# Rotating an 8192 x 8192 matrix: 16 KB load pieces and merged store reads in place of 4 KB pieces

## The chip, the cores and the metric

One core of one Trainium2 chip runs the kernel. The metric is the time of one execution on the device, in microseconds (us). All times are medians of several executions; readings of a profile are from one of these executions.

Ratios are computed as the mean time of one kernel's runs over the mean of the other kernel's runs in the same rounds, so they are not quite the ratio of the medians quoted beside them.

## The reference

```python
x = np.random.randn(8192, 8192).astype(np.float32)   # 268.4 MB
def reference(x, k):          # k == 1
    return np.rot90(x, k)     # out[i, j] = x[j, 8191 - i]
```

A rotation moves data and computes nothing. Each byte must be read once and written once: 268.4 MB in and 268.4 MB out.

## The kernel before

Rotating means transposing and reversing. The kernel loads rows into SBUF, reverses each group of 128 columns on VectorE (DVE), transposes 128 x 128 blocks on TensorE (PE) into PSUM, copies from PSUM to SBUF on ScalarE (ACT), and stores. Loads are issued on the SP queue, stores on the ACT queue; the same 16 DMA engines serve both.

```python
QT = 4; PT = 4; S = 512; K = 2
# a_pool, r_pool, o_pool: 3 buffers each, of 16 KB per partition; psum: 2 buffers
for RB2 in range(n_rb2):
    for CB2 in range(n_cb2):                    # macro tile of 1024 x 1024
        for t in range(K):                      # a load: 512 rows x 1024 columns, 2 MB
            a_big = a_pool.tile([P, QT, K * S], dt, tag="a_big")
            src = x[...].rearrange("(q r) c -> r q c", q=QT)
            nc.sync.dma_start(out=a_big[:], in_=src)          # 4 KB pieces
            ar_big = r_pool.tile([P, QT, K * S], dt, tag="ar_big")
            nc.vector.tensor_copy(out=ar_big..., in_=a_big...[:, :, ::-1])
        for s in range(K):
            o_big = o_pool.tile([P, PT, K * S], dt, tag="o_big")
            for t in range(K):
                # ... 16 transposes into psum_t ...
                nc.scalar.copy(o_big[:, :, t * S : (t + 1) * S], psum_t[:])
            dst = out[...].rearrange("(p m) f -> m p f", p=PT)
            nc.scalar.dma_start(out=dst, in_=o_big[:])        # 4 KB pieces
```

A "piece" here is one contiguous run that a DMA moves: in this kernel 1,024 floats, 4 KB, on both sides of every load and every store.

## Time and profile before

| | before |
|---|---|
| time | 1286.25 us (1285.63 to 1286.27) |
| PE, ACT, DVE busy | 56%, 37%, 23% |
| DMA busy | 0.9 or more in all but the last slice |
| rate in mid-span | 421 GB/s, flat |

The first fence is from the page of the kernel before. In the slices, each digit is the busy share of one fortieth of the span in tenths, and the GB/s line has the rate of the same slices. Section 3 has packets, MB and packet time as a share of the 16 engines' span for each queue: q1 holds the loads, q10 the stores.

```profile
DMA  9999999999999999999999999999999999999998
GB/s 382 422 421 421 421 421 422 421 421 421 421 421 421 421 421 421 421 422 421 420 421 421 421 421 421 421 421 421 422 420 420 421 421 422 421 421 421 421 421 361
DMA packets 135208, 537.48 MB, mean 418 GB/s; under 512 B 4096, under 2 KB 4096, under 8 KB 135168
q1 hardware_dynamic: 67584, 268.44, 50.9%
q10 hardware_dynamic: 67584, 268.44, 50.9%
DMA 88%; DVE 8%; PE 2%; ACT 1%; issue 0%; DVEq 0%; SPq 0%
a_big<-in_x_dram SPq DMA_DIRECT2D x128, 2048.0 KB, 27.4
out_dram<-o_big ACTq DMA_DIRECT2D x128, 2048.0 KB, 26.1
```

The kernel is bound by DMA. No slice but the last has free DMA time, no compute engine is busy for even 60% of the span, and the chain of work that ended last is 88% DMA. The 67,584 packets per queue are 65,536 data packets of 4,096 B and 2,048 completion writes. So only two things can make it faster: a higher rate of the DMA engines while they run, and less idle time at the two ends.

### The profile page before, as it was taken

How to read it: one execution, taken by the hardware profiler on the slowest of the kernel's cores; microseconds unless marked ns; L12 is line 12 of the kernel's file. 1: busy time of each engine (PE TensorE's matmuls, PEld its weight loads, DVE VectorE, ACT ScalarE, POOL GpSimd, SP SyncE). 2: the span in 40 equal slices, each digit the busy share in tenths (PEclk: the TensorE clock that was granted, in tenths of full speed). 3: DMA queues.
4: the chain of work that ended last, by engine and by line, in shares of the span. 5: the costliest groups of instructions: out<-in, count | busy, mean ns of one | idle time of the engine just before them, and what ended most of it. 6: DMA issues, size and time to landing. Idle time of an engine off the chain costs nothing.

```text
span 1284.6 us, 9394 instructions
## 1 busy us (share of the span) xinstructions
PE 718.8 (56%) x4096; PEld 662.7 (52%) x4096; DVE 293.6 (23%) x128; ACT 471.1 (37%) x257; POOL 0.7 (0%) x6
## 2 busy tenths in 40 slices
PE   5465564556555565456554565555646556465553
PEld 5455464555544555456454464555645456455553
DVE  2222222222222222222222222222222222222221
ACT  3334433343333433343333433334333343334433
POOL 0000000000000000000000000000000000000000
PEclk9666766776767767776777767767677766776776
DMA  9999999999999999999999999999999999999998
GB/s 382 422 421 421 421 421 422 421 421 421 421 421 421 421 421 421 421 422 421 420 421 421 421 421 421 421 421 421 422 420 420 421 421 422 421 421 421 421 421 361
DMA packets 135208, 537.48 MB, mean 418 GB/s; under 512 B 4096, under 2 KB 4096, under 8 KB 135168
## 3 DMA queue, kind: packets, MB, share of 16 engines
q1 hardware_dynamic: 67584, 268.44, 50.9%
q10 hardware_dynamic: 67584, 268.44, 50.9%
q8 instruction: 32, 0.52, 0.1%
q14 instruction: 8, 0.07, 0.0%
HBM read 268.44 MB, written 268.44 MB: 418 GB/s over the span
## 4 chain that ended last, share of the span: by engine, by line
DMA 88%; DVE 8%; PE 2%; ACT 1%; issue 0%; DVEq 0%; SPq 0%
DMA a_big<-in_x_dram 88%; DVE ar_big L60 8%; PE psum_t L76 2%; ACT o_big L81 1%; DVEq L60 0%; SPq L55 0%
## 5 line engine op out<-in xcount | busy, mean ns | idle before, releaser
L76 PE MATMUL psum_t<-ident,ar_big 128*128 128x128 f32 x4096 | 718.8, 354 | 552.7 <-ACT o_big L81 354.4
L76 PEld LDWEIGHTS psum_t<-ident,ar_big 128*128 128x128 f32 x4096 | 662.7, 188 | 608.5 <-ACT o_big L81 389.5
L81 ACT COPY o_big<-psum_t 128x2048 f32<-128x2048 f32 x256 | 469.9, 1868 | 801.5 <-DMA out_dram<-o_big 771.6
L60 DVE COPY ar_big<-a_big 128x4096 f32<-128x4096 f32 x128 | 293.6, 2294 | 970.6 <-DMA a_big<-in_x_dram 816.4
L81 ACT ACT_TABLE_LOAD x1 | 1.3, 1283 | 0.7 <-PEq L104 0.7
masks.py:199 POOL TENSOR_SCALAR_AFFINE_SELECT ident<-ident 128x128 f32<-128x128 f32 x1 | 0.3, 292 | 0.1
masks.py:197 POOL MEMSET ident<- 128x128 f32 x1 | 0.2, 204 | 0.3 <-POOLq L104 0.3
L104 POOL MEMSET const-bfloat16-1.0<- 128x1 bf16 x1 | 0.1, 102 | 0.0
L104 POOL MEMSET const-uint8-127<- 128x1 uint8 x1 | 0.1, 102 | 0.0
L104 POOL MEMSET const-float32-0.0<- 128x1 f32 x1 | 0.1, 98 | 0.2 <-issue 0.2
L104 POOL MEMSET const-float32-1.0<- 128x1 f32 x1 | 0.1, 98 | 0.0
## 6 DMA issues: line engine op xcount, KB each, us to landing
a_big<-in_x_dram SPq DMA_DIRECT2D x128, 2048.0 KB, 27.4
out_dram<-o_big ACTq DMA_DIRECT2D x128, 2048.0 KB, 26.1
```

The costliest lines, as they stand in the source:

```text
L60: nc.vector.tensor_copy(out=ar_big.rearrange("r q (b m) -> r (q b) m", m=P), in_=rev_src,)
L76: nc.tensor.transpose(psum_t[:, w, q * P : (q + 1) * P], ar_big[:, q, col0 : col0 + P], ident,)
L81: nc.scalar.copy(o_big[:, :, t * S : (t + 1) * S], psum_t[:])
L104: nc = _bacc.Bacc("TRN2", target_bir_lowering=False, num_devices=1)
```

## The change

The intent is fewer and larger DMA pieces. A macro tile is now 512 rows x 4096 columns, so a load fetches 16 KB of one row per partition in one piece. Stores shrink to 1 MB, four output rows of 2 KB per partition. The four rows lie side by side in SBUF, and a hook that runs over the finished program rewrites the store's source so that the 8 KB are read as one piece, while the destination keeps four rows of 2 KB.

```diff
+R = 512
+C = 4096
+RT = R // P          # 4 row tiles
+G = 2048 // R        # 4 column blocks to a store
+def whole_reads(nc):
+    ...               # for each DMA instruction:
+    ap = [list(d) for d in src.ap]
+    if len(ap) == 3 and ap[2][0] == 1 and ap[1][0] == ap[2][1]:
+        ap = [ap[0], [1, 1], [1, ap[1][1] * ap[2][1]]]
+        block.instructions[n] = copy.replace(
+            ins, ins=[copy.replace(src, ap=ap)], ant_dge_precooked=False)
...
-    a_pool bufs=3, r_pool bufs=3, o_pool bufs=3          (16 KB each)
+    a_pool bufs=2 (16 KB), r_pool bufs=2 * RT (16 KB), o_pool bufs=5 (8 KB)
...
+    for r0 in range(0, N, R):
+        for c0 in range(0, M, C):
+            for t in range(RT):
+                a = a_pool.tile([P, C], dt, tag="a")
+                nc.sync.dma_start(out=a[:], in_=x[r0 + t*P : r0 + (t+1)*P, c0 : c0 + C])
+                ar = r_pool.tile([P, C], dt, tag="ar")      # reversed by DVE as before
+            for g0 in range(0, CG, G):
+                o = o_pool.tile([P, G, R], dt, tag="o")
+                # ... 16 transposes, one ACT copy of [128, 2048] ...
+                dst = out[top : top + G*P, r0 : r0 + R].rearrange("(g m) f -> m g f", g=G)
+                nc.scalar.dma_start(out=dst, in_=o[:])
```

The counts of matmuls (4096), DVE copies (128) and ACT copies (256) stay. Stores go from 128 of 2 MB to 256 of 1 MB.

More of the change, by code (lines that the diff above doesn't have):

```diff
@@ L2 @@
+import copy
 from contextlib import ExitStack
@@ L10 @@
 P = 128
+R = 512
+C = 4096
+RT = R // P
+CG = C // P
+G = 2048 // R
+PW = 2048 // R
+def whole_reads(nc):
+    for fn in nc.m.functions:
+        for block in fn.blocks:
+            for n, ins in enumerate(block.instructions):
+                if not isinstance(ins, mybir.InstDMACopy):
+                    continue
+                src = ins.ins[0]
+                ap = [list(d) for d in src.ap]
+                if len(ap) == 3 and ap[2][0] == 1 and ap[1][0] == ap[2][1]:
+                    ap = [ap[0], [1, 1], [1, ap[1][1] * ap[2][1]]]
+                    block.instructions[n] = copy.replace(
+                        ins,
+                        ins=[copy.replace(src, ap=ap)],
+                        ant_dge_precooked=False,
+                    )
 @with_exitstack
@@ L22 @@
     assert k == 1, f"only k=1 supported, got {k}"
+    nc.at_finalize(whole_reads)
     N, M = x.shape
     dt = x.dtype
-    QT = 4
-    PT = 4
-    S = 512
-    K = 2
-    n_rb2 = N // (K * S)
-    n_cb2 = M // (K * S)
     consts = ctx.enter_context(tc.tile_pool(name="consts", bufs=1))
@@ L37 @@
     make_identity(nc, ident)
-    a_pool = ctx.enter_context(tc.tile_pool(name="a_pool", bufs=3))
-    r_pool = ctx.enter_context(tc.tile_pool(name="r_pool", bufs=3))
-    o_pool = ctx.enter_context(tc.tile_pool(name="o_pool", bufs=3))
-    psum_pool = ctx.enter_context(tc.tile_pool(name="psum", bufs=2, space=bass.MemoryType.PSUM))
-    for RB2 in range(n_rb2):
-        for CB2 in range(n_cb2):
-            c_base = CB2 * K * S
-            r_base = RB2 * K * S
-            ar_list = []
-            for t in range(K):
-                a_big = a_pool.tile([P, QT, K * S], dt, tag="a_big")
-                src = x[
-                    r_base + t * S : r_base + (t + 1) * S, c_base : c_base + K * S
-                ].rearrange("(q r) c -> r q c", q=QT)
-                nc.sync.dma_start(out=a_big[:], in_=src)
-                ar_big = r_pool.tile([P, QT, K * S], dt, tag="ar_big")
-                nblk = QT * K * S // P
-                rev_src = a_big.rearrange("r q (b m) -> r (q b) m", m=P)[:, :, ::-1]
+    a_pool = ctx.enter_context(tc.tile_pool(name="a_pool", bufs=2))
@@ new lines @@
+    r_pool = ctx.enter_context(tc.tile_pool(name="r_pool", bufs=2 * RT))
+    o_pool = ctx.enter_context(tc.tile_pool(name="o_pool", bufs=5))
+    psum_pool = ctx.enter_context(
+        tc.tile_pool(name="psum", bufs=2, space=bass.MemoryType.PSUM)
+    )
+    for r0 in range(0, N, R):
+        for c0 in range(0, M, C):
+            rows = []
+            for t in range(RT):
+                a = a_pool.tile([P, C], dt, tag="a")
+                nc.sync.dma_start(
+                    out=a[:], in_=x[r0 + t * P : r0 + (t + 1) * P, c0 : c0 + C]
+                )
+                ar = r_pool.tile([P, C], dt, tag="ar")
@@ L60 @@
                 nc.vector.tensor_copy(
-                    out=ar_big.rearrange("r q (b m) -> r (q b) m", m=P),
-                    in_=rev_src,
-                )
-                ar_list.append(ar_big)
-            for s in range(K):
-                cb = K * CB2 + s
-                o_big = o_pool.tile([P, PT, K * S], dt, tag="o_big")
-                for t in range(K):
-                    psum_t = psum_pool.tile([P, PT, QT * P], mybir.dt.float32)
-                    ar_big = ar_list[t]
-                    for p in range(PT):
-                        w = PT - 1 - p
-                        col0 = s * S + p * P
-                        for q in range(QT):
+                    out=ar.rearrange("r (b m) -> r b m", m=P),
@@ L76 @@
+                    in_=a.rearrange("r (b m) -> r b m", m=P)[:, :, ::-1],
+                )
+                rows.append(ar)
+            for g0 in range(0, CG, G):
+                o = o_pool.tile([P, G, R], dt, tag="o")
+                for h in range(0, G, PW):
+                    ps = psum_pool.tile([P, PW, R], mybir.dt.float32)
+                    for w in range(PW):
+                        col = (g0 + h + w) * P
+                        for t in range(RT):
                             nc.tensor.transpose(
-                                psum_t[:, w, q * P : (q + 1) * P],
@@ L78 @@
-                                ar_big[:, q, col0 : col0 + P],
+                                ps[:, PW - 1 - w, t * P : (t + 1) * P],
+                                rows[t][:, col : col + P],
                                 ident,
                             )
-                    nc.scalar.copy(o_big[:, :, t * S : (t + 1) * S], psum_t[:])
-                top = N - S - cb * S
-                dst = out[top : top + S, r_base : r_base + K * S].rearrange(
-                    "(p m) f -> m p f", p=PT
+                    nc.scalar.copy(o[:, G - PW - h : G - h, :], ps[:])
@@ L86 @@
+                top = M - c0 - (g0 + G) * P
+                dst = out[top : top + G * P, r0 : r0 + R].rearrange(
+                    "(g m) f -> m g f", g=G
                 )
-                nc.scalar.dma_start(out=dst, in_=o_big[:])
+                nc.scalar.dma_start(out=dst, in_=o[:])
 _INS = ['x', 'k']
```

## The prediction

> **What bounds it now.** The 16 DMA engines. The page's slices show a DMA busy share of 0.9 or more throughout and a flat 421 GB/s from the second slice to the last but one; PE is busy 56%, ACT 37%, DVE 23% of the span. The chain of waits is 88% load DMA. So only the rate per DMA engine and the idle DMA at both ends count.
>
> **The rate, from the trace's packet records.** All data packets are 4,096 B. One takes 159 ns, a completion write 9 ns. While only the load queue runs (the first 23 us of data) the rate is 410 GB/s, which is 16 x 2 MB/(32 x 159 + 9 ns): packets follow each other without overlap. With both queues running, 421 GB/s means one 4 KB packet per 155.8 ns on each engine. The Trainium skill, "DMA: Bandwidth & Descriptors", section "Where 436 GB/s comes from", gives a ceiling of 435.2 GB/s, or 150.6 ns per 4 KB; its section "Why small descriptors are slow" names a fixed cost per packet. This trace agrees with both: 5.2 ns over the ceiling with two queues, 8.4 ns with one. An 8,192 B instruction-fetch packet took 307 ns at the start, under 2 x 159.
>
> **What the change does.** Matmuls (4096), DVE copies (128) and evictions (256, 1.87 us) stay as they are. Loads stay 128 x 2 MB, but in 16 KB pieces rather than 4 KB. Stores become 256 x 1 MB: 8 KB read pieces, but 2 KB output rows. 128 more store issues (0.38 us each) go to ACT, which has 800 us idle: free.
>
> Sum per 4 KB with two queues, if the cost is per read piece: loads 150.6 + 5/4, stores 150.6 + 5/2, some 0.2 for completions: mean about 152.7 ns against 155.8, 2.0% less. 8,192 x 3.1 ns = 25 us, all on the critical path. I take off about 3 us: a 16 KB load packet against an 8 KB store packet should give loads the larger share, so they run ahead, fill their buffers and leave stretches in which only stores run, at the dearer one-queue cost. Ends: the first store comes about 7 us later (four loads, not two, go first), but loads fill that time; the tail ends in smaller stores. Both near zero. Compute keeps pace in store-only stretches: 16 transposes take 1.97 us at full clock, an ACT copy with its issue about 2.3 us, a 1 MB store about 2.5 us. At half clock 16 transposes take 3.6 us, but five output buffers cover that.
>
> If the cost is per written piece instead, stores take 150.6 + 10, the mean is about 156.4 ns, and the time is 1290 to 1303.
>
> **Prediction: 1263 us, 80% range 1247 to 1294. Faster by over 2%: 0.40; within 2%: 0.52; slower by over 2%: 0.08.**
>
> **What would show it.** Right: steady rate 428 to 431 GB/s; fewer, larger packets (16 KB loads near 610 ns, not four of 159); loads share above half in some slices; DMA still 0.9 or more in every slice; the chain still DMA; PE, ACT and DVE totals unchanged. Wrong: rate at or below 421 GB/s, store packets of 2 KB at 80 ns or more each; or DMA gaps in mid-span with ACT waiting for PE at half clock.
>
> **What would make it wrong.** 2 KB output rows that cost HBM or the write side more than 4 KB rows; a 16 KB row still cut into 4 KB pieces, so that nothing is gained on loads; load buffers (two, not three) leaving the load queue empty after each 2.3 us DVE copy while stores cannot fill the gap; coarser macro tiles (8 MB) making loads and stores alternate; a real ceiling under 435 GB/s, so that little of the 5 ns is recoverable.

## The result, and the profile after

| | before | after |
|---|---|---|
| median | 1285.98 us (1285.63 to 1286.27, 4 runs) | 1279.92 us (1278.93 to 1282.31, 4 runs) |
| ratio | | 0.9955, 95% interval 0.9941 to 0.9969 |
| rate, 200 to 1100 us | 420.9 GB/s | 423.8 GB/s |
| lost at both ends against that rate | 7.4 us | 9.9 us |

The change is faster by 0.45%, where 1.8% was forecast. The third row is bytes moved in 200 to 1100 us of the span, from the trace's packet records. The fourth is the span less the time that all bytes would take at that rate.

The same lines of the page, for the changed kernel:

```profile
DMA  9999999999999999999999999999999999999998
GB/s 364 424 425 424 426 423 424 426 425 424 424 425 427 422 426 424 424 426 426 422 422 425 422 425 424 422 422 424 427 417 427 420 423 426 417 428 421 425 422 352
DMA packets 55339, 537.51 MB, mean 421 GB/s; under 512 B 6144, under 2 KB 6144, under 8 KB 6144
q10 hardware_dynamic: 36864, 268.45, 50.5%
q1 hardware_dynamic: 18432, 268.44, 49.6%
DMA 91%; PE 4%; ACT 3%; issue 0%; DVE 0%; ACTq 0%; SPq 0%
a<-in_x_dram SPq DMA_DIRECT2D x128, 2048.0 KB, 12.7
out_dram<-o ACTq DMA_DIRECT2D x256, 1024.0 KB, 20.9
```

Three readings. The pieces are what the change wanted: 16,384 load packets of 16 KB and 32,768 store packets of 8 KB (36,864 less 4,096 completion writes), so a store with four output rows does count as one packet. The rate rose by under 1% only, and it is no longer flat: slices go from 417 to 428 GB/s. And a load now lands 12.7 us after its issue, not 27.4, while a store still needs 20.9 us for half of the bytes: the loads get more than their share.

The share can be read from the DMA view of single stretches. This is the changed kernel from 622 to 646 us of the span (packets, MB, share of the 16 engines):

```profile
q1 hardware_dynamic: 437, 6.39, 62.8%
q10 hardware_dynamic: 511, 3.73, 37.4%
```

and this is the same view from 653 to 661 us:

```profile
q10 hardware_dynamic: 461, 3.36, 101.2%
q1 hardware_dynamic: 1, 0.00, 0.0%
```

With both queues running, loads move nearly twice the bytes of stores. Then no load runs at all. The Trainium skill, "DMA: Bandwidth & Descriptors", section "Queues, rings and completion order", says that each DMA engine takes turns between the queues that have work, a packet at a time. This trace agrees: packets of 16 KB against packets of 8 KB give 6.39 against 3.73 MB. The records do not name the engine, but they can be chained into 16 engines, because each one starts a few ns before another ends. In the chains of the changed kernel from 200 to 1100 us, 8,868 of some 10,200 unbroken runs of load records on one engine are a single record, so a turn here is one piece. The loads run ahead until their buffers are full, and the view of waits shows on what they then wait (engine, line, what it waited for: us in total, times, longest). Before:

```profile
DVE ar_big L60 <- DMA a_big<-in_x_dram: 816.4, 108, 8.6
DVE ar_big L60 <- PE psum_t L76: 154.2, 20, 8.6
```

After:

```profile
DVE ar L83 <- DMA a<-in_x_dram: 500.6, 71, 10.9
DVE ar L83 <- PE ps L96: 443.0, 30, 21.2
```

The DVE copy now waits 443 us for PE to free row buffers, up to 21.2 us at a time; while it waits, no load buffer comes free.

Sorting the span by microseconds, from the packet records with each packet's bytes spread over its time: in the changed kernel 726 us have both queues at about 2:1 and run at 426.0 GB/s, 292 us have stores alone at 418.7, and 220 us lie between at 420.7. In the kernel before, 1223 us have both queues at 1:1 and run at 420.4. The bounds between these sorts are a choice; other bounds move them by some tens of us.

### The profile page after: what moved, and what is told of

The parts are those of the page before. It is cut to its first block, busy times and chain, and to the rows that moved or that the text cites. A ratio compares the mean times of both kernels' runs of the same rounds, so it can differ in the third digit from the quotient of the medians.

```text
span 1278.2 us, 9636 instructions
## 1 busy us (share of the span) xinstructions
PE 708.0 (55%) x4096; PEld 641.3 (50%) x4096; DVE 291.2 (23%) x128; ACT 479.0 (37%) x257; POOL 0.7 (0%) x6
## 3 DMA queue, kind: packets, MB, share of 16 engines
q10 hardware_dynamic: 36864, 268.45, 50.5%
## 4 chain that ended last, share of the span: by engine, by line
DMA 91%; PE 4%; ACT 3%; issue 0%; DVE 0%; ACTq 0%; SPq 0%
DMA out_dram<-o 90%; PE ps L96 4%; ACT o L101 3%; DMA a<-in_x_dram 2%; DVE ar L83 0%; ACTq L107 0%; ACTq L101 0%; SPq L77 0%
## 5 line engine op out<-in xcount | busy, mean ns | idle before, releaser
L96 PE MATMUL ps<-ident,ar 128*128 128x128 f32 x4096 | 708.0, 348 | 557.2 <-ACT o L101 531.6
L96 PEld LDWEIGHTS ps<-ident,ar 128*128 128x128 f32 x4096 | 641.3, 183 | 623.5 <-ACT o L101 596.2
L101 ACT COPY o<-ps 128x2048 f32<-128x2048 f32 x256 | 477.7, 1868 | 787.4 <-DMA out_dram<-o 708.7
L83 DVE COPY ar<-a 128x4096 f32<-128x4096 f32 x128 | 291.2, 2293 | 943.6 <-DMA a<-in_x_dram 500.6
## 6 DMA issues: line engine op xcount, KB each, us to landing
a<-in_x_dram SPq DMA_DIRECT2D x128, 2048.0 KB, 12.7
out_dram<-o ACTq DMA_DIRECT2D x256, 1024.0 KB, 20.9
```

Of the source, the lines that this page charges most:

```text
L83: nc.vector.tensor_copy(out=ar.rearrange("r (b m) -> r b m", m=P), in_=a.rearrange("r (b m) -> r b m", m=P)[:, :, ::-1],)
L96: nc.tensor.transpose(ps[:, PW - 1 - w, t * P : (t + 1) * P], rows[t][:, col : col + P], ident,)
L101: nc.scalar.copy(o[:, G - PW - h : G - h, :], ps[:])
```

## The experiments

Two theories stood at the start. **Cuts**: the forecast counted only read pieces, and each row that a store piece is cut into on the write side costs too. **Alternation**: loads of 16 KB and stores of 8 KB drive each other into stretches with one queue, which the forecast took off at 3 us. A third was that compute and the coarse macro tile hold the rate down.

### The store reads not merged

```diff
-    nc.at_finalize(whole_reads)
```

> The changed kernel without the merging of the store reads: each store reads 2 KB pieces as it writes 2 KB rows. Theory A (the fixed cost is per read piece, about 5 ns with two queues and 8.4 ns with one): store records of 2 KB at about 84 ns, loads get 8/9 of the mixed rate, store-only rate near 2048*16/84 = 390 GB/s, time 1305 to 1335 us. Theory B (the cost is per written piece, so merging reads bought nothing): time within 0.3% of the changed kernel, about 1280 us, and store-only rate still near 418 GB/s.

Measured: 1330.24 us, ratio 1.034 (1.0322 to 1.0357), right result.

```profile
DMA packets 153643, 537.51 MB, mean 404 GB/s; under 512 B 6144, under 2 KB 6144, under 8 KB 137216
q10 hardware_dynamic: 135168, 268.45, 53.0%
q1 hardware_dynamic: 18432, 268.44, 48.9%
```

A store packet of 2 KB takes 84 ns in the packet records, four of them 336 ns; the merged packet of 8 KB took 314 ns. So the cost follows read pieces for the most part, as the forecast had it, and merging is worth 50 us here: without it the change would have been a loss of 3.4%. Not all of the 50 us is the price of pieces: with packets of 2 KB against 16 KB, the records show about 480 us of stores alone at about 400 GB/s.

### Loads in 8 KB pieces

```diff
-nc.sync.dma_start(out=a[:], in_=x[r0 + t*P : r0 + (t+1)*P, c0 : c0 + C])
+for j in range(0, C, 2048):
+    nc.sync.dma_start(out=a[:, j : j + 2048], in_=x[..., c0 + j : c0 + j + 2048])
```

> The changed kernel with each load row fetched as two DMAs of 8 KB pieces, so that load and store packets are equal. Theory A (alternation: 16 KB load packets against 8 KB store packets give loads two thirds, they run ahead, and the 292 us of store-only stretches at 418.7 GB/s follow): shares go to one half each, store-only time in mid-span falls under 60 us, rate near the 426 GB/s of the mixed stretches nearly all the time, 1266 to 1273 us. Theory B (alternation is harmless, the size of the load piece is what counts): 8 KB load pieces cost 1.3 ns more per 4 KB of load, time 1281 to 1287 us.

Measured: 1281.03 us, ratio 0.9962 (0.9947 to 0.9977), right result. The store-only time fell from 292 to 32 us and the rate became even (most slices 422 to 425), yet the time is that of the changed kernel. Theory B's number came out. As the cuts below show, it is not its reason alone: here the cuts are what is left to see.

### Macro tiles of 1024 x 2048

```diff
-R = 512
-C = 4096
+R = 1024
+C = 2048
-    a_pool bufs=2
+    a_pool bufs=4
```

> Macro tiles of 1024 rows x 2048 columns: 8 KB load pieces, 8 KB store reads, output rows of 4 KB rather than 2 KB. Against the run with 8 KB loads and 2 KB output rows this changes the length of the written row. Theory A (a cut on the write side adds cost: the 8 KB store record of 315 ns over 309 ns in the first stretch is that cut): store records near 310 ns and 0.3 to 1% faster than the run with 2 KB rows, about 1258 to 1268 us. Theory B (written pieces are free): the same time as that run within 0.2%.

Measured: 1279.04 us, ratio 0.9944 (0.9929 to 0.9958), right result. Store records fell to 310 ns, as theory A said, but the time came down by 0.15% only, which is theory B's time. From 100 to 500 us the rate was 426.6 GB/s; from 1100 to 1200 us it was 418.1, and 12.0 us were lost at the ends.

### Stores in 16 KB pieces

```diff
-G = 2048 // R          # o_pool bufs=5, r_pool bufs=2 * RT
+G = 4096 // R          # o_pool bufs=3, r_pool bufs=2 * RT - 1
```

> The changed kernel with stores of 2 MB that read 16 KB pieces for eight 2 KB rows, so both queues move 16 KB packets (3 output buffers of 16 KB, 7 row buffers). Theory A (alternation costs, and the cost is per read piece): equal shares, hardly any store-only stretch, rate 427 to 431 GB/s, 1256 to 1268 us. Theory B (alternation harmless): only the saving per store piece, about 1 ns per 4 KB of store, 1274 to 1279 us. If the write cuts dominate: store records of 16 KB near 628 ns, no gain over the run with 8 KB loads.

Measured: 1280.40 us, ratio 0.9957 (0.9936 to 0.9977), right result. The shares are even and the mid-span rate is 425.5 GB/s, under the forecast. Store records are 624.6 ns against 613 for loads of the same size: eight rows of 2 KB cost. The plain copy with the same pieces and rows, below, has 426.0, so the cuts explain the rate. 14.6 us were lost at the ends, against 7.1 in that copy.

### Plain copies: the queues without compute

To settle the sum, four kernels copy instead of rotating. They share 12 buffers of 16 KB between loads and stores and use no compute engine. Their outputs are wrong, which doesn't matter for the times.

```diff
+for each block of 128 x 4096 floats:
+    a = pool.tile([P, 4096], dt, tag="a")          # 12 buffers
+    nc.sync.dma_start(out=a..., in_=x...)          # pieces of 4, 8 or 16 KB
+    nc.scalar.dma_start(out=out..., in_=a...)      # the same pieces, or rows of 2 KB
```

> No rotation: a plain copy of the input with no compute, so the result is wrong on purpose; it measures the two DMA queues by themselves. Pieces of 4 KB both ways, shapes as in the kernel before. If compute and its waits cost the kernel before nothing in mid-span, the mid-span rate is again 421 GB/s (155.7 ns per 4 KB on each engine).

> Plain copy, wrong on purpose: pieces of 8 KB both ways, no cuts. Theory A (a fixed cost of 5.2 ns per piece with two queues over a ceiling of 435 GB/s): 153.2 ns per 4 KB, 428 GB/s in mid-span. Theory B (some ceiling near 426 GB/s binds whatever the piece): at most 426 to 427 GB/s, and the 16 KB copy the same.

> Plain copy, wrong on purpose: pieces of 16 KB both ways, no cuts. Theory A (fixed cost per piece): 151.9 ns per 4 KB, 431 GB/s in mid-span. Theory B (a ceiling near 426 GB/s): 426 to 427 GB/s, no more than with 8 KB pieces.

> Plain copy to rotated block places, wrong on purpose: loads of 16 KB pieces, stores that read 16 KB and write eight 2 KB rows. Theory of the cuts (each cut of a store piece costs about 1.9 ns, as the 624.6 ns against 612 ns records of the run with 16 KB stores suggest): store records 622 to 627 ns against 611 in the 16 KB copy without cuts, mid-span rate 1% below that copy. Rival (the longer store records come from compute or from waiting for the load queue, not from the cuts): the same rate and records as the 16 KB copy.

The fences show the stretch from 200 to 1100 us of the 4 KB, the 8 KB and the 16 KB copy, and of the 16 KB copy whose stores write eight rows of 2 KB, in this order. The last two numbers of a line are the DMA share and GB/s.

```profile
200.00:1100.00 900.00, 0.00 (x0) 1.00 1.02 422
```

```profile
200.00:1100.00 900.00, 0.00 (x0) 1.00 1.01 428
```

```profile
200.00:1100.00 900.00, 0.00 (x0) 1.00 1.01 431
```

```profile
200.00:1100.00 900.00, 0.00 (x0) 1.00 1.01 426
```

| copy | time | mid-span | per 4 KB on one engine |
|---|---|---|---|
| 4 KB both ways | 1281.05 us | 421.5 GB/s | 155.5 ns |
| 8 KB both ways | 1262.88 us | 428.0 GB/s | 153.1 ns |
| 16 KB both ways | 1253.21 us | 431.3 GB/s | 152.0 ns |
| 16 KB, stores in eight 2 KB rows | 1268.58 us | 426.0 GB/s | 153.8 ns |

The last column is 16 x 4,096 B over the rate. The first three rows fit one line: 150.8 ns plus 4.7 ns per piece (155.5, 153.15 and 152.0). The forecast's piece cost (5.2 ns over 150.6) was right, and theory A of these runs holds; there is no lower ceiling near 426 GB/s. The cuts are right too: eight written rows instead of one cost 15 us of time.

### Is it the cut, or the short row? And the cuts taken out of the changed kernel

```diff
 # 16 KB copy: four rows of 4 KB instead of eight of 2 KB
-top, left = n // 16 * 1024, n % 16 * 512      # g=8
+top, left = n // 8 * 512, n % 8 * 1024        # g=4
```

> The plain copy with 16 KB store reads, now written as four 4 KB rows instead of eight 2 KB rows (wrong on purpose). Theory A (a price per cut, 13.1 ns over seven cuts): three cuts give records of 616 to 617 ns and 429 GB/s in mid-span. Theory B (short rows of 2 KB are what is slow, 4 KB rows are free): records of 611 ns and 431 GB/s.

Measured: 1257.45 us, 429.7 GB/s, store records of 614.8 ns (611 uncut, 624.1 with eight rows). Its output is wrong, which doesn't matter for the time. From the rates, the pair of a load and a store piece takes 2 x 16,384 x 16/rate: 1215.7 ns uncut, 1220.1 with three cuts, 1230.7 with seven. That is 1.5 ns per cut with 4 KB rows and 2.1 ns with 2 KB rows. Most of it goes by the cut, and short rows add to it: between the theories, nearer to A.

```diff
 # changed kernel: each store writes its 8 KB in one piece; wrong on purpose
-dst = out[top : top + G*P, r0 : r0 + R].rearrange("(g m) f -> m g f", g=G)
-nc.scalar.dma_start(out=dst, in_=o[:])
+nc.scalar.dma_start(out=out[top : top + P, left : left + 2048],
+                    in_=o.rearrange("m g f -> m (g f)"))
```

> The changed kernel, in which each store writes its 8 KB per partition as one piece to a contiguous place rather than as four 2 KB rows; the result is wrong on purpose, everything else (macro tiles, loads, buffers, compute) is as in the changed kernel. Theory A (three cuts per store piece cost 4 to 6 ns and take back about half of the gain): mid-span rate 426 to 428 GB/s, store records near 309 rather than 314 ns, 1266 to 1272 us. Theory B (the gain went into the alternation of loads and stores and into the ends, not the cuts): within 0.3% of the changed kernel, 1277 to 1283 us.

Measured: 1279.05 us (1275.55 to 1282.69), ratio 0.9944 (0.9919 to 0.997). **Theory A failed here.** The cuts cost less when taken away, as far as that goes: store records fell from 314.3 to 310.8 ns and the store-only stretches rose from 418.7 to 425.1 GB/s. But the two-queue stretches stayed at 425.7, those between fell to 419.7, and the slices swing further than before:

```profile
GB/s 352 420 429 427 428 425 425 426 426 427 422 426 426 413 426 426 428 426 427 424 428 426 426 426 425 414 429 425 422 425 424 427 419 416 428 420 425 425 417 341
```

So taking the cuts away does not raise the rate. The packet records show where the gain went: as the stores became shorter, the mean load record grew from 615.7 to 619.8 ns.

### Only the merged reads, on the kernel before

```diff
+    nc.at_finalize(whole_reads)          # store: 16 KB read, four rows of 4 KB written
```

> The kernel before with nothing changed but its store reads merged: 16 KB read pieces for four 4 KB rows; loads stay in 4 KB pieces. By the piece and cut costs: loads 5 ns, stores (5 + 3 x 1.9)/4 = 2.7 ns over the ceiling per 4 KB, mean 154.6 ns, 424 GB/s, about 1277 us if stores and loads still overlap well. Rival: store packets four times the size of load packets take the queue from the loads, so loads wait, load-only stretches at 410 GB/s follow, and the time is 1283 us or more.

Measured: 1287.46 us, ratio 1.0012 (0.9997 to 1.0026), right result. The rival is right. Store packets of 16 KB against load packets of 4 KB take the turn for four times as long; the stores drain, and 447 us have loads alone at 410.9 GB/s. The cheaper store pieces are given back in full. This is the alternation from the other side, and the clearest case of it: nothing changed here but the size of one queue's pieces.

### Smaller tiles at the ends

```diff
+cuts = [512, 512, 1024, 2048, 2048, 2048] in the first row block, reversed in the last
```

> Search for a version that beats both: macro tiles of 1024 x 2048 as before, but the first and the last are split into column widths of 512, 512 and 1024, so that the first store comes earlier and the last stores wait less. The run with 1024-row tiles lost 12.0 us against its mid-span rate at the two ends, the plain 8 KB copy 6.4 us. If the ends are what is left to gain: 2 to 5 us faster than that run, 1273 to 1277 us. If the short pieces at the ends cost as much as they save: 1278 to 1281 us.

Measured: 1293.63 us, ratio 1.0058 (1.0043 to 1.0073), right result: a miss. Both ends became slower. The last row block holds the slices 373, 388 and 312, where the kernel with even tiles had 418, 411 and 331:

```profile
GB/s 311 413 426 426 427 427 426 427 428 426 426 427 426 427 427 426 426 427 427 426 425 427 422 423 426 424 426 425 424 424 422 425 423 417 426 419 427 373 388 312
```

### Unequal pieces without compute, and the square completed

```diff
 # 16 KB copy, but each buffer stored as two DMAs of 8 KB pieces
+for j in range(0, 4096, 2048):
+    nc.scalar.dma_start(out=out[..., c0 + j : c0 + j + 2048], in_=a[:, j : j + 2048])
```

> Plain copy, wrong on purpose: 16 KB load pieces, 8 KB store pieces, no cuts, no compute. If the piece costs add up as in the 4, 8 and 16 KB copies, also for unequal pieces: 152.5 ns per 4 KB, 429 to 430 GB/s. If unequal packets in the two queues cost by themselves: 424 to 426 GB/s, like the changed kernel with uncut stores.

> Plain copy to rotated block places, wrong on purpose: the changed kernel's own transfers (16 KB load pieces, 8 KB store reads cut into four 2 KB rows) without its compute. By pieces and cuts: 153.9 ns per 4 KB, 425.5 to 427 GB/s in mid-span and 1267 to 1271 us. What the changed kernel loses beyond that (423.8 GB/s and 1279.9 us) is then due to how its loads and stores follow each other. If it gives 424 GB/s and less, the pieces and cuts explain the whole mid-span.

Measured, both wrong: 1279.81 us and 424.8 GB/s without cuts, as its second alternative said; 1280.03 us and 423.2 GB/s with each 8 KB written as four 2 KB rows, the changed kernel's own transfers. The second is under the 425.5 to 427 that pieces and cuts give, without any compute. The stretch from 200 to 1100 us of the copy without cuts and of the copy with cuts, in this order:

```profile
200.00:1100.00 900.00, 0.00 (x0) 1.00 1.01 425
```

```profile
200.00:1100.00 900.00, 0.00 (x0) 1.00 1.01 423
```

This is the main result. With 16 KB pieces both ways the copy took 1253.2 us, with 8 KB both ways 1262.9, and with 16 KB one way and 8 KB the other 1279.8, although by its pieces it should lie between the two. It has no compute, no macro tile and no cuts. Of the 20 us by which its profiled span exceeds the mean of the two, 14 are rate and 6 are lost at the ends.

The packet records show where the rate goes, though not why. About 234 us have stores alone, but these are not slow. Here are the queue in one such stretch, from 285 to 289 us, and the rate in it and in the next of this length:

```profile
q10 hardware_dynamic: 240, 1.70, 100.9%
```

```profile
285.00:289.00 4.00, 0.00 (x0) 1.00 1.01 426
324.00:328.00 4.00, 0.00 (x0) 1.00 1.01 426
```

All 45 such stretches of 3 us or more in mid-span have a mean of 427 GB/s, more than the whole. The loss lies at the changes between the two states: aligned on the 29 restarts of the loads that a count of single microseconds finds from 100 to 1150 us, the total rate dips to 414 GB/s at the restart and to 416 some 6 us later, and reaches 430 in between and after. No engine stands idle: in the chains of records the 16 engines idle 5 us together, of 16 x 900. Single records take longer instead. The median load record is 611 ns, as in the 16 KB copy, but 694 of 11,587 are over 5% longer, and they make up 7.4 of the 10 us that the rate costs from 200 to 1100 us. They cluster at the changes, without being confined to them: 65% of them, but 42% of all load records, lie within 2 us of a microsecond with less than half loads. The mean records of that stretch:

| run | load record, 16 KB | store record, 8 KB |
|---|---|---|
| copies with equal pieces of 16 KB and of 8 KB | 611 ns | 309 ns |
| copy with 16 KB against 8 KB, no cuts | 621 | 310 |
| the same with four rows to a store piece | 617 | 315 |
| changed kernel | 616 | 314 |
| changed kernel, uncut stores | 620 | 311 |

Cuts lengthen the store records, unequal pieces the load records; without cuts the load records lengthen more.

```diff
 # changed kernel with 8 KB loads AND uncut stores (wrong on purpose)
```

> The changed kernel with 8 KB load pieces (equal packets, no alternation) and uncut 8 KB store pieces written contiguously; wrong on purpose. It completes a square with the changed kernel (alternating, cut: 1279.9 us), the run with uncut stores (alternating, uncut: 1279.05 us) and the run with 8 KB loads (equal, cut: 1281.0 us). Theory A (two losses that hide each other: cuts cost, and the handovers between load and store stretches eat what is saved when only the cuts go): mid-span 427 to 428 GB/s, 1266 to 1272 us. Theory B (compute and its waits hold every version with this macro tile near 424 GB/s): 1277 to 1282 us.

Measured: 1279.85 us, ratio 0.9948 (0.9931 to 0.9964). Theory B's time came out, but neither theory fits the whole of it. These are its slices:

```profile
GB/s 374 414 395 427 427 427 425 427 428 426 427 426 427 427 427 427 426 424 423 423 425 426 423 425 425 425 423 424 425 413 419 424 423 424 424 424 423 423 423 339
```

From 100 to 500 us it ran at 426.6 GB/s, near theory A's number; from then on most slices have 421 to 426, with 84 us of loads alone at 415.3 GB/s. So equal pieces let it start right, but the two queues drifted out of step. Load records lengthen here too, to a mean of 312.5 ns against 309.1 in the 8 KB copy, so unequal pieces are not the only way to get them. The 8 KB copy, with the same uncut pieces and no compute, took 1262.9 us: with equal pieces, the compute and its macro tiles cost 17 us that no run here takes apart.

### A third load buffer

```diff
-    a_pool bufs=2, r_pool bufs=2 * RT
+    a_pool bufs=3, r_pool bufs=2 * RT - 1
```

> The changed kernel with three load buffers instead of two, and seven row buffers instead of eight for room; right result. Theory A (the dips to 410 GB/s at each restart of the loads, and the dip in load rate after the second load, come from a load queue that holds only one or two loads): the dips shrink, the first 50 us lose about 1 to 2 us less, 1274 to 1279 us. Theory B (the dips come with any restart): within 0.2% of the changed kernel.

Measured: 1277.54 us (1276.83 to 1278.31), ratio 0.9933 (0.9918 to 0.9948), right result. The dips at the restarts stayed (407 GB/s), and so did mid-span (423.7 GB/s). What went is a loss at the start. These are the stretches from 10 to 30 us of the changed kernel and of this one, in this order (busy times of PE, PEld, DVE, ACT, POOL; clock, DMA share, GB/s):

```profile
10.00:30.00 20.00, 5.28 (x21) 4.11 (x22) 7.18 (x4) 0.17 (x1) 0.00 (x0) 1.00 1.00 377
```

```profile
10.00:30.00 20.00, 6.92 (x29) 5.76 (x30) 9.55 (x5) 1.82 (x1) 0.00 (x0) 1.00 1.00 429
```

While only loads run, two buffers do not keep the queue full: each must wait for its 2.3 us DVE copy. The ends cost 7.0 us instead of 9.9, which accounts for the 2.4 us gained. It is the lowest median of a right kernel, but the intervals of the two ratios overlap.

### Freeing row buffers column group by column group

```diff
 # reversed rows kept as [128, 256] pieces; the next tile's rows take the pieces
 # in the order in which PE frees them
+here = [free[t * NC : (t + 1) * NC] for t in range(RT)]
+free = [here[t][c] for c in range(NC) for t in range(RT)]
```

That is the form of the second kernel below; the first uses two such sets.

> Search, right result: tiles of 1024 x 2048, equal 8 KB load and store pieces with one cut, and the reversed rows kept in pieces of 256 columns that are freed column group by column group, so that every 1 MB stored frees room for 1 MB loaded, as in the plain copies. Theory A (handovers at macro-tile boundaries eat the gain): the load share stays even, mid-span 426.5 to 427.5 GB/s against 425.5 of the 1024-row run, 1265 to 1273 us. Theory B (the dips come from something else in the compute, or 2048 small DVE copies now bind): 1277 us or more.

> Search, right result: the same freeing by column group, which now lets one 16 MB tile of 1024 x 4096 suffice, with equal 16 KB load and store pieces and three cuts per store piece, as in the plain copy that ran at 429.7 GB/s and 1257 us. Theory A (equal large pieces and even flow are what counts): mid-span 428 to 429.7 GB/s, 3 to 8 us lost at the ends with two buffers each side, 1260 to 1270 us. Theory B (one tile and two buffers leave gaps in DMA at each tile's end): 1275 us or more, with slices below 415 GB/s.

Measured: 1281.25 us (ratio 0.996, 0.9944 to 0.9977) and 1283.58 us (0.9982, 0.9967 to 0.9997), right results. Both missed. The slices of the first:

```profile
GB/s 389 424 426 427 425 426 427 426 427 426 426 427 426 426 427 426 426 427 426 426 427 427 426 427 427 426 424 424 424 426 424 425 424 421 417 423 411 416 366 337
```

It holds 425 to 427 GB/s from the third slice to the 26th, which is what pieces and cuts give, and then decays; 16.3 us were lost at the ends. So the macro tile that frees its buffers all at once is not the only cause of the drift.

One trace of that drift can be measured. Each DMA has 16 completion writes, one to an engine, and it is complete with the last. The table has the mean time from the first to the last engine's completion of one DMA, in the stretches 100 to 300, 500 to 700 and 900 to 1100 us, beside the rate there:

| kernel | 100-300 us | 500-700 us | 900-1100 us |
|---|---|---|---|
| 16 KB copy | 431.3 GB/s, 0.9 us | 431.2, 1.5 | 431.2, 1.8 |
| 16/8 KB copy | 424.3, 5.5 | 425.3, 10.8 | 424.2, 12.8 |
| before | 421.0, 1.9 | 420.9, 3.5 | 420.8, 5.9 |
| changed | 424.4, 4.2 | 424.2, 5.5 | 423.0, 6.1 |
| changed, equal and uncut | 426.5, 3.0 | 424.6, 6.6 | 421.2, 6.6 |
| freed by column group (8 KB) | 426.3, 3.7 | 426.6, 9.1 | 424.2, 13.8 |

The unequal copy is far apart from the first stretch, and most runs that fall short of their pieces are far apart too. But the distance is no measure of the loss: the last kernel of the table still runs at 426.6 GB/s with its engines 9.1 us apart, and the unequal copy with cuts went from 421 to 424 GB/s while its distance grew from 4.9 to 9.3 us. Nor do engines that are ahead run out of work: the chains show hardly any idle time (above). Whether the distance has a part in the longer load records is not shown.

## Why the prediction was wrong

- **"What bounds it now: the 16 DMA engines" was right.** The copy with the changed kernel's own transfers and no compute takes 1280.0 us, the kernel 1279.9. (In the formula for one queue, "16 x 2 MB" should read 2 MB, which all 16 engines share.)
- **The piece cost was right.** The forecast read 5.2 ns per piece out of one rate and a ceiling of 435.2 GB/s in the Trainium skill ("DMA: Bandwidth & Descriptors", section "Where 436 GB/s comes from"). Copies of 4, 8 and 16 KB give 4.7 ns over 150.8 ns, and 431.3 GB/s at best, close under that ceiling.
- **"If the cost is per read piece" was mostly right, and incomplete.** Unmerged reads cost 50 us, a part of it through stores alone, so reads count most; but cuts on the write side are not free: 15 us in the 16 KB copy with eight rows. In equal 8 KB pieces the sum fits: 153.1 ns of the 8 KB copy plus three cuts of 2.1 ns in one store piece, spread over 16 KB, is 154.7; the run with 8 KB loads has 154.8 (423.4 GB/s).
- **The step that failed is the allowance: "I take off about 3 us" for unequal packets, with nothing for the cuts.** That loads take two thirds, fill their buffers and leave store-only stretches was forecast and came. Its price was not. Without compute or cuts, the copy with 16 KB against 8 KB takes 1279.8 us, while equal pieces of 8 and of 16 KB take 1262.9 and 1253.2, mean 1258: about 22 us for being unequal. And the price is not where the forecast put it, in a dearer store-only stretch (427 GB/s there, 424.8 in all), but in longer load records, most frequent around the handovers.
- **In the changed kernel itself the cuts are the larger part.** With records of 611 and 309 ns it would run mid-span at about 429 GB/s, the forecast's own rate (an estimate from the records). A load piece and two store pieces take 15 ns more than those 1,229 ns: 10.5 in the stores, through the cuts, and 4.7 in the loads. Over the run that is an estimated 11 and 5 us; with 2.5 us at the ends and less the 3 allowed, it makes up most of the 17 us by which the forecast missed.
- **The losses do not add, and no run of the full kernel got them back.** In the changed kernel, cuts out: 1279.05; pieces equal: 1281.0; both: 1279.85. With unequal pieces, what the cuts give back goes into longer load records; with equal pieces and cuts, the cuts explain the rate; with neither, the queues drift apart after 500 us. Kernels with equal pieces take longer than copies with the same pieces: 1279.85 against 1262.9 us (8 KB, uncut), 1280.4 against 1268.6 (16 KB, eight rows), 1283.6 against 1257.5 (16 KB, four rows). With unequal pieces kernel and copy agree to 1 us. So the third theory, that compute and the macro tile hold the rate down, is excluded for the changed kernel's own transfers only. Why the equal kernels drift where equal copies do not, and why load records lengthen, stays open.
- **"Ends: both near zero" was off by 2.5 us** (9.9 against 7.4 us lost), for the reason listed under what would make it wrong: two load buffers. The third buffer took it back.
- **Of the signs named, the slices gave the answer at once.** 428 GB/s was reached in single slices only; the load share above half was there.

## What to carry to other kernels

When two queues share the DMA engines, do not expect the saving of larger pieces in one queue to add up: in plain copies an unequal pair ran slower than the smaller of the two sizes used both ways. In the full kernel, though, equal pieces alone brought nothing, so this is a risk to price and not yet a recipe. Count a piece by its longer side and add a small price for each cut on the other; merging the reads of a store is worth much when the alternative is 2 KB pieces (50 us here). And test a claim about transfers with a plain copy of the same pieces: it needs no compute, and it tells what the transfers alone can reach. It does not tell what the kernel will reach.

## What the Trainium skill lacked or had wrong

- "DMA: Bandwidth & Descriptors", section "Why small descriptors are slow", gives a fixed cost of about 3 cycles per packet. Here it is 4.7 ns per piece with both queues running, and the records of one 4 KB piece (159 ns) stand 8.4 ns over its share of the ceiling of 435.2 GB/s. The page does not tell the two apart.
- No page says what a store costs whose read side is one piece and whose write side is several: 1.5 ns per cut for rows of 4 KB, 2.1 ns for rows of 2 KB, and one packet record for the whole.
- The same page, section "Queues, rings and completion order", has the turn-taking by packets of typically 9 to 17 descriptors, and the table of the gpsimd path in its section "SWDGE vs HWDGE vs iDMA" calls a packet at most 4,096 B "preferably". Here, on queues of SP and ACT, a 16 KB piece is one record of 611 ns and one turn (8,868 of some 10,200 runs of load records on one engine are single), so a queue's share follows its piece size (6.39 against 3.73 MB in 24 us).
- No page says that unequal pieces in the two queues lower the total rate: 424.8 GB/s for 16 KB against 8 KB, where 8 KB both ways gives 428.0 and 16 KB both ways 431.3.
- No page says how far apart the engines' completions of one DMA can drift: 1.8 us late in the run of the 16 KB copy, 12.8 us late in that of the unequal one.
